# Undivided softmax probabilities, and their reciprocal sums sent through memory into the gate

## The chip, the cores and the metric

The kernel runs on one core of one Trainium2 chip. The metric is device time in microseconds, from the launch to the end of the program on the core; lower is better. The engines are TensorE (PE, with its weight loads shown as PEld), VectorE (DVE), ScalarE (ACT), GpSimd (POOL) and SyncE (SP), which here issues every DMA of the steady stage. Each engine works through its own list of instructions in order and waits on semaphores for the others.

## The reference

One encoder layer over 4096 tokens of width 1024. What matters here is the attention half: 32 blocks of 128 queries, 8 query heads that share 2 key heads, and a window of three key blocks.

```python
h = rmsnorm(x, pre_norm_g)
q, k, v, g_a, u_p, g_p = split(h @ w_in)
s = q k^T * scale + bias            # a 128-query block against 3 key blocks of 128
m = max(max(s), sink)
p = exp(s - m)
p = p / (sum(p) + exp(sink - m))    # the softmax with a sink
a = (p @ v) * silu(g_a)             # the gate
mixed = concat(a, pool(u_p) * silu(g_p)) @ w_out
out = x + rmsnorm(mixed, post_norm_g)
```

The division by the sum may stand before p @ v (on the probabilities) or after it (on the gate, since both multiply the same row). The change moves it from the one place to the other.

## The kernel before

The program has two stages. The first, to about 490 us, prepares weights, the pooling half and the gate `ga` = silu(g_a), which it writes to memory (`ga_scr`). The second, the attention stage, walks the 32 blocks from the last to the first, two blocks (a unit `u` of 256 tokens) at a time. Its middle part is a loop of 13 units, with blocks 27 to 2; blocks 31 to 28 and 1 to 0 have orders written out by hand.

Every float32 operand of TensorE is carried as two float16 numbers, a high part (a rounded copy, written by ACT) and a low part (the rest, written by DVE or POOL), and a product is three matmuls: high by high, high by low, low by high.

A block `b` has two passes, `half` 0 and 1, of four heads each. In a pass:

- `scores`: PE writes the logits of four heads into PSUM (`s`);
- `logits` (four, DVE): adds the bias and finds the row's maximum, into `p`. With the first, POOL copies the sink into one column of `p` (the sink copy, L1330);
- `exps` (four, ACT): exponentials in place, with their sums `den`;
- `denominators` (DVE): two tiny operations make `rd` = 2^14 / sum;
- `probs` (four, ACT, one head each): the high part of p * rd into `pn`; `rests` (four, DVE): the low part;
- `turn` (SP): one transposing DMA of `pn` into `pt`, which PE needs for `values` (p @ v).

`values` leaves its result in two PSUM tiles (`o`, and `p` in a bank of the general pool). `copy_o` (ACT) and `gate` (DVE, two operations, of which the second multiplies by the gate `gb`, which `load_ga` has fetched) make the attention output `at`. `sums`, `high` and `low` then form operands for seven `product`s per unit, named "11", "22", "12", "s1" to "s4", which PE multiplies with `w_out`; they accumulate in the same general PSUM banks (acc0, acc1, acc2) that `proj_k`, `proj_v` and `proj_q` use. `add`, `gain` (mostly POOL), `square` (ACT), `mean` (a tiny DVE operation and a power on POOL, `rs`), `residual` (DVE) and `store` finish a unit. `load_x` fetches 1 MB of operands for the unit after next.

What stands in which order on an engine is set by due times: each step is entered into a plan with a time, the plan is sorted by it, and each engine's list follows that order. The loop orders PE's work so: `scores(b,0)`, product "s4", `proj_k`, `proj_v`, `values(b+1)`, `scores(b,1)`, products "22", "11", "s2", "12" for an odd block; `scores(b,0)`, two projections of q, `values(b+1)`, `scores(b,1)`, two projections of q, products "s3", "s1" for an even one. `softmax(b, half, t)` enters a pass's steps:

```python
due(t + 4.5 + 0.6 * i, probs, b, half, i)
due(t + 5.1 + 0.62 * i, rests, b, half, i)
...
due(t + 7.8, turn, b, half)
```

In the even block `load_x` is due 2.1 after the second pair of q projections, which was just ahead of that pass's `turn`. The product "22" of the next odd block needs the low part `y22`, which POOL makes late in the even block's last passes, behind a `gain` and the power `rs`.

Of the kernel before, what the change touches and what calls it, by code (L numbers as in the profile page):

```python
# [8 lines left out]
F32 = mybir.dt.float32  # L9
# [125 lines left out]
def hybrid_layer(ctx: ExitStack, tc, io, out):  # L135
# [46 lines left out]
    ga_scr = dram.tile([NB, P, 4, P], F32, name="ga_scr")  # L182
    wb_scr = dram.tile([6, P, 2, D], F16, name="wb_scr")
# [1095 lines left out]
    pt, p_t, nm_t, den_t, rd_t, pn_t = {}, {}, {}, {}, {}, {}  # L1279

# [40 lines left out]
    def logits(b, half, i):  # L1321
# [20 lines left out]
    def exps(b, half, i):  # L1342
# [6 lines left out]
            scale=-1.0, accum_out=den_t[b, half][:, hh : hh + 1],  # L1349
        )  # L1350

    def denominators(b, half):
        den = den_t.pop((b, half))
        nc.vector.tensor_scalar(
            out=den, in0=den, scalar1=1.0 / P_SCALE, scalar2=None, op0=ALU.mult
        )
        nc.vector.reciprocal(rd_t[b, half], den)
# [5 lines left out]
    def probs(b, half, i):  # L1363
        nk = len(keys(b)) * P
        if i == 0:
# [3 lines left out]
        nc.scalar.activation(  # L1369
            prob_view(b, half)[:, 0, i], p_t[b, half][:, i, :nk], AF.Copy,  # L1370
            scale=rd_t[b, half][:, i : i + 1],
        )

    def rests(b, half, i):
        nk = len(keys(b)) * P
        pn4 = prob_view(b, half)
        nc.vector.scalar_tensor_tensor(  # L1377
            out=pn4[:, 1, i], in0=p_t[b, half][:, i, :nk], scalar=rd_t[b, half][:, i : i + 1],
            in1=pn4[:, 0, i], op0=ALU.mult, op1=ALU.subtract,
# [372 lines left out]

    now = [0.0]
# [439 lines left out]
```

## Time and profile before

| | |
|---|---|
| median of 3 runs | 1162.19 us (1161.15 to 1162.24) |
| the profiled execution | 1162.76 us, of which the span of its instructions is 1161.0 us |
| PE busy | 1146.3 us, 99% of the span |
| PEld busy | 873.5 us, 75% |
| DVE busy | 947.8 us, 82% |
| ACT busy | 717.7 us, 62% |
| POOL busy | 313.7 us, 27% |
| DMA, all queues | 228.36 MB, 197 GB/s on the mean |

The busy share of an engine is the share of the span in which it had an instruction in flight; matmuls overlap, so a PE that is busy 99% of the time is one that hardly ever stood still, and no more. In the timeline rows below, the columns are start (us), length (us), engine, line, operation, what it writes <- what it reads, shape and count; a bracket tells how long the engine stood idle before and for whom. `SPq` rows are DMA issues: their length is the time SP spent on the issue, not the transfer.

### The profile page before, as it was taken

How to read it: one execution, taken by the hardware profiler on the slowest of the kernel's cores; microseconds unless marked ns; L12 is line 12 of the kernel's file. 1: busy time of each engine (PE TensorE's matmuls, PEld its weight loads, DVE VectorE, ACT ScalarE, POOL GpSimd, SP SyncE). 2: the span in 40 equal slices, each digit the busy share in tenths (PEclk: the TensorE clock that was granted, in tenths of full speed). 3: DMA queues.
4: the chain of work that ended last, by engine and by line, in shares of the span. 5: the costliest groups of instructions: out<-in, count | busy, mean ns of one | idle time of the engine just before them, and what ended most of it. 6: DMA issues, size and time to landing. Idle time of an engine off the chain costs nothing. (4 is left out here: it accounts for less than half of the span.)

```text
span 1161.0 us, 32325 instructions
## 1 busy us (share of the span) xinstructions
PE 1146.3 (99%) x13420; PEld 873.5 (75%) x13420; DVE 947.8 (82%) x1875; ACT 717.7 (62%) x1485; POOL 313.7 (27%) x310
## 2 busy tenths in 40 slices
PE   8999999999999999999999999999999999999997
PEld 7998888888888888886667676576666767667653
DVE  6889988988799974568878888878887888887886
ACT  6876556536654542257676776676667677667772
POOL 0001120211111010201524433532533443353231
PEclk8999999999999999999999999999999999999999
DMA  9645575867667664299975886788777688777885
GB/s 344 217 128 180 174 259 183 285 229 238 227 190 225 206 179 134 76 289 242 250 185 144 197 211 143 200 202 177 177 196 184 148 198 215 140 196 165 178 216 143
DMA packets 301683, 228.36 MB, mean 197 GB/s; under 512 B 219568, under 2 KB 259504, under 8 KB 296928
## 3 DMA queue, kind: packets, MB, share of 16 engines
q1 hardware_dynamic: 301536, 226.30, 72.5%
q8 instruction: 105, 1.72, 0.6%
q14 instruction: 42, 0.34, 0.1%
HBM read 114.68 MB, written 60.34 MB: 151 GB/s over the span
## 5 line engine op out<-in xcount | busy, mean ns | idle before, releaser
L689 PEld LDWEIGHTS <-wq 128*128 128x128 f16 x4104 | 401.6, 98 | 50.4 <-DVE wq L310 2.6
L689 PE MATMUL y<-xt,wq 128*128 128x256 f16 x1512 | 203.3, 273 | 0.1
L1347 ACT ACTIVATE p<-p,nm 128x385 f32<-128x385 f32 (+1 forms) x256 | 152.9, 599 | 36.5 <-POOL p L1330 20.3
L1273 PE MATMUL aq<-xb,xb 128*128 128x256 f16 x1024 | 173.4, 273 | 0.2 <-DVE mo L1715 0.2
L1273 PEld LDWEIGHTS <-xb 128*128 128x128 f16 x1536 | 150.1, 98 | 26.4 <-issue 8.0
L1676 PE MATMUL ms<-wo,ys 128*128 128x512 f16 x720 | 163.7, 379 | 0.0
L1377 DVE SCALAR_TENSOR_TENSOR pn<-p,rd,pn 128x384 f16<-128x384 f32 (+1 forms) x256 | 157.6, 667 | 5.9 <-ACT pn L1369 5.9
L1336 DVE CUSTOM_DVE_ANT_0 p<-s,nt,nsink 128x384 f32<-128x384 f32 (+1 forms) x256 | 156.0, 666 | 2.0 <-PE s L1313 2.0
L1273 PE MATMUL aq<-xb,xt 128*128 128x256 f16 x512 | 139.6, 273 | 0.4 <-issue 0.4
L1369 ACT ACTIVATE pn<-p,rd 128x384 f16<-128x384 f32 (+1 forms) x256 | 134.8, 596 | 4.4 <-issue 1.1
L307 POOL TENSOR_TENSOR yt<-yt,sg 128x512 f32<-128x512 f32 (+2 forms) x32 | 51.0, 1594 | 301.6 <-DVE yt L310 214.8
L1676 PEld LDWEIGHTS <-ys 128*128 128x128 f16 x720 | 68.1, 98 | 83.9 <-POOL ys L1582 4.8
L1676 PE MATMUL m<-wo,y 128*128 128x512 f16 x540 | 121.8, 379 | 0.0
L1676 PEld LDWEIGHTS <-y 128*128 128x128 f16 x540 | 51.4, 98 | 63.5 <-ACT at L1543 2.9
L1273 PE MATMUL kv<-xb,xb 128*128 128x256 f16 x512 | 86.7, 273 | 0.0
L1710 POOL TENSOR_TENSOR mo<-mo,gpost 128x512 f32<-128x512 f32 x39 | 63.7, 1634 | 84.4 <-ACT jkb L1699 83.2
L1273 PEld LDWEIGHTS <-xt 128*128 128x128 f16 x768 | 75.1, 98 | 10.6 <-issue 0.8
L689 PE MATMUL plain<-xb,wq 128*128 128x256 f16 x576 | 68.0, 276 | 2.1 <-DVE wq L310 2.0
L1273 PE MATMUL kv<-xb,xt 128*128 128x256 f16 x256 | 69.8, 273 | 0.0
L689 PE MATMUL v<-xt,wq 128*128 128x256 f16 x504 | 68.6, 273 | 0.1
L689 PE MATMUL v<-xb,wq 128*128 128x256 f16 x504 | 68.6, 273 | 0.0
L689 PE MATMUL y<-xb,wq 128*128 128x256 f16 x504 | 68.6, 273 | 0.0
(221 smaller groups left out, 1854.3 us busy)
## 6 DMA issues: line engine op xcount, KB each, us to landing
nt<-in_xT SPq DMA_DIRECT2D x28, 512.0 KB
x_scr<-xb SPq DMA_DIRECT2D x14, 1024.0 KB
xb<-x_scr SPq DMA_DIRECT2D x14, 1024.0 KB
xr<-in_x SPq DMA_DIRECT2D x28, 512.0 KB
out<-xr SPq DMA_DIRECT2D x28, 512.0 KB
xn<-in_x SPq DMA_DIRECT2D x27, 512.0 KB
ga_scr<-cc SPq DMA_DIRECT2D x64, 128.0 KB
raw<-in_w_out SPq DMA_DIRECT2D x16, 512.0 KB
```

The costliest lines, as they stand in the source:

```text
L307: eng.tensor_tensor(out=out, in0=in0, in1=in1, op=op)
L689: nc.tensor.matmul(b[:, s], wq[:, slot[q, op], wv, s, k, :], x[:, xv, k, :], start=(first and k + s + wv + xv == 0), stop=(last and k == H ...
L1273: nc.tensor.matmul(acc, w[:, j, k, :], x[:, kh, v, kt, :], start=(n == 0), stop=(n == 3 * KT - 1),)
L1336: nc.vector.tensor_tensor_reduce(out=p_t[b, half][:, hh, :nk], in0=s_t[jj][:, gg, :nk], in1=bias[:, h, lo : lo + nk], scale=negc[:, h : h ...
L1347: nc.scalar.activation(p[:, hh, : nk + 1], p[:, hh, : nk + 1], AF.Exp, bias=nm_t[b, half][:, hh : hh + 1], scale=-1.0, accum_out=den_t[b, ...
L1369: nc.scalar.activation(prob_view(b, half)[:, 0, i], p_t[b, half][:, i, :nk], AF.Copy, scale=rd_t[b, half][:, i : i + 1],)
L1377: nc.vector.scalar_tensor_tensor(out=pn4[:, 1, i], in0=p_t[b, half][:, i, :nk], scalar=rd_t[b, half][:, i : i + 1], in1=pn4[:, 0, i], op0= ...
L1676: nc.tensor.matmul(z_t[u, tag], y[:, k, yi, :], wo[o][:, wi, k, :], start=(n == 0 and acc is None), stop=(n == 3 * HK - 1), skip_group_che ...
L1710: eng.tensor_tensor(out=mo, in0=mo, in1=gpost[:, cs], op=ALU.mult)
```

## The change

- `probs` and `rests` no longer divide: they scale the exponentials by the constant 2^14. Since no per-head scalar is left, one operation takes two heads (768 columns where there were 384), so a pass has two of each instead of four.
- The sums of both passes of a block go into one tile `den` of 8 columns. Once a block, after its second pass, DVE takes one reciprocal and transposes it in 32 x 32 pieces (`rec`); SP writes it to memory with four small DMAs (`keep_rows`, 8 partitions by 128 bytes each) and reads it back with two (`load_rows`, each a row of 2 KB repeated over 64 partitions) into `rdb`, a spare part of the tile XB0; POOL multiplies the gate `gb` by it (`divide`, 128 x 512 float32). `gate` then reads a gate that is already divided.
- The due times of `probs`, `rests` and `turn` are earlier, by 0.4, 0.1 and 0.9 us in the plan; `load_rows` is due at t + 8.0 and `divide` at t + 15.0.

```diff
+    rec = [pb1.tile([P, 32], F32, name=f"rec{i}") for i in range(2)]
+    rdb = XB0[:, 6 * D :].bitcast(F32).rearrange("p (i h q) -> p i h q", i=2, h=4)
...
-    def denominators(b, half):
-        den = den_t.pop((b, half))
-        nc.vector.tensor_scalar(
-            out=den, in0=den, scalar1=1.0 / P_SCALE, scalar2=None, op0=ALU.mult
-        )
-        nc.vector.reciprocal(rd_t[b, half], den)
+    def denominators(b):
+        nc.vector.reciprocal(rec[0][:, :NH], den_t.pop(b))
+        nc.vector.transpose(out=rec[1], in_=rec[0])
+
+    def keep_rows(b):
+        for i in range(4):
+            nc.sync.dma_start(
+                rd_scr[b, :, 32 * i : 32 * i + 32], rec[1][32 * i : 32 * i + NH, :]
+            )
+
+    def load_rows(b):
+        for g in range(2):
+            rows = rd_scr[b, 4 * g : 4 * g + 4, :].rearrange("(o h) q -> o h q", o=1)
+            nc.sync.dma_start(
+                rdb[64 * g : 64 * g + 64, b % 2], rows.to_broadcast([64, 4, P])
+            )
+
+    def divide(b):
+        ga = ga_t[b]
+        nc.gpsimd.tensor_tensor(out=ga, in0=ga, in1=rdb[:, b % 2], op=ALU.mult)
...
-        nc.scalar.activation(
-            prob_view(b, half)[:, 0, i], p_t[b, half][:, i, :nk], AF.Copy,
-            scale=rd_t[b, half][:, i : i + 1],
-        )
+        hs = slice(2 * i, 2 * i + 2)
+        nc.scalar.mul(prob_view(b, half)[:, 0, hs], p_t[b, half][:, hs, :nk], P_SCALE)
...
-            out=pn4[:, 1, i], in0=p_t[b, half][:, i, :nk], scalar=rd_t[b, half][:, i : i + 1],
-            in1=pn4[:, 0, i], op0=ALU.mult, op1=ALU.subtract,
+            out=pn4[:, 1, hs], in0=p_t[b, half][:, hs, :nk], scalar=P_SCALE,
+            in1=pn4[:, 0, hs], op0=ALU.mult, op1=ALU.subtract,
...
-            due(t + 4.5 + 0.6 * i, probs, b, half, i)
-            due(t + 5.1 + 0.62 * i, rests, b, half, i)
-        due(t + 4.3, denominators, b, half)
-        due(t + 7.8, turn, b, half)
+        for i in range(2):
+            due(t + 4.1 + 0.75 * i, probs, b, half, i)
+            due(t + 5.0 + 0.95 * i, rests, b, half, i)
+        if half:
+            due(t + 4.3, denominators, b)
+            due(t + 4.9, keep_rows, b)
+            due(t + 8.0, load_rows, b)
+            due(t + 15.0, divide, b)
+        due(t + 6.9, turn, b, half)
```

The hand-written orders at both ends get the same steps, with `load_rows` due at the later of 0.1 after `turn` and 2.5 after `denominators`, and `divide` 2.5 after that.

Three places show what the change does to the order. The first is SP's list in the second pass of an even block (here block 20 of unit 10), from the `turn` of its first pass (`pt20_0`) to the `turn` of the next block (`pt19_0`); `xr` are the residual's inputs, `gb20` the gate, `xb1<-x_scr` is `load_x`. Before:

```order
L1386 DMA_TRANSPOSE pt20_0_10490<-pn20_0_10355 128x24x128
L1723 DMA xr22_10492<-in_x 128x1024
L1723 DMA xr23_10494<-in_x 128x1024
L1460 DMA gb20_10554<-ga_scr_97 128x512
L1259 DMA xb1_68<-x_scr_95 128x4096
L1386 DMA_TRANSPOSE pt20_1_10593<-pn20_1_10568 128x24x128
L1743 DMA out_0<-xr22_10492 128x1024
L1386 DMA_TRANSPOSE pt19_0_10767<-pn19_0_10723 128x24x128
```

And the same place of SP's list after the change:

```order
L1403 DMA_TRANSPOSE pt20_0_10369<-pn20_0_10287 128x24x128
L1745 DMA xr22_10423<-in_x 128x1024
L1745 DMA xr23_10425<-in_x 128x1024
L1482 DMA gb20_10483<-ga_scr_97 128x512
L1362 DMA rd_scr_98<-rec1_6088 8x32 x4
L1403 DMA_TRANSPOSE pt20_1_10521<-pn20_1_10492 128x24x128
L1260 DMA xb1_68<-x_scr_95 128x4096
L1369 DMA xb0_66<-rd_scr_98 64x512 x2
L1765 DMA out_0<-xr22_10423 128x1024
L1403 DMA_TRANSPOSE pt19_0_10687<-pn19_0_10652 128x24x128
```

The four small writes come in ahead of the `turn`; `load_x`, which stood ahead of it, now stands behind it, and the two `load_rows` stand behind `load_x`.

The second place is POOL's list from the sink copy of block 19's first pass to the low part `y12` (unit 11 is being finished, unit 10 prepared). Before:

```order
L1330 COPY p19_0_10677<-nsink_87 128x4
L1710 TENSOR_TENSOR mo11_1_10179<-mo11_1_10179,gpost_6084 128x512
L1733 TENSOR_TENSOR rs11_1_10715<-ms11_1_10713,mhalf_72 128x1
L1710 TENSOR_TENSOR mo11_0_10178<-mo11_0_10178,gpost_6084 128x512
L1733 TENSOR_TENSOR rs11_0_10759<-ms11_0_10757,mhalf_72 128x1
L1582 TENSOR_TENSOR y22_10_10762<-yf0_10_10224,y22_10_10762 128x4x128
L1582 TENSOR_TENSOR y12_10_10764<-yf1_10_10343,y12_10_10764 128x4x128
```

POOL's list at the same place after the change (`gb20<-gb20,xb0` is the `divide` of block 20; `xb0` holds `rdb`):

```order
L1333 COPY p19_0_10607<-nsink_87 128x4
L1732 TENSOR_TENSOR mo11_1_10116<-mo11_1_10116,gpost_6085 128x512
L1755 TENSOR_TENSOR rs11_1_10645<-ms11_1_10643,mhalf_72 128x1
L1375 TENSOR_TENSOR gb20_10483<-gb20_10483,xb0_66 128x512
L1732 TENSOR_TENSOR mo11_0_10115<-mo11_0_10115,gpost_6085 128x512
L1755 TENSOR_TENSOR rs11_0_10685<-ms11_0_10683,mhalf_72 128x1
L1604 TENSOR_TENSOR y22_10_10689<-yf0_10_10161,y22_10_10689 128x4x128
L1604 TENSOR_TENSOR y12_10_10691<-yf1_10_10279,y12_10_10691 128x4x128
```

The `divide`, which waits for the two `load_rows`, has come in ahead of a `gain`, a power and the low parts `y22` and `y12`.

The third place is ACT's list in both passes of block 20, from the exponentials of the first to the `probs` of the second. Before:

```order
L1347 ACTIVATE p20_0_10338,den20_0_10336<-p20_0_10338,nm20_0_10335 128x385 x4
L1262 ACTIVATE q9_0_10352<-aq9_0_10285 128x512
L1369 ACTIVATE pn20_0_10355<-p20_0_10338,rd20_0_10337 128x384 x4
L1543 ACTIVATE at21_10438<-o21_10360,gaf_78 128x512
L1578 CAST y11_10_10496<-at21_10438 128x4x128
L1347 ACTIVATE p20_1_10550,den20_1_10548<-p20_1_10550,nm20_1_10547 128x385 x4
L1262 ACTIVATE q9_1_10565<-aq9_1_10498 128x512
L1369 ACTIVATE pn20_1_10568<-p20_1_10550,rd20_1_10549 128x384 x4
```

ACT's list there after the change:

```order
L1350 ACTIVATE p20_0_10274,den20_10273<-p20_0_10274,nm20_0_10272 128x385 x4
L1388 ACTIVATE pn20_0_10287<-p20_0_10274 128x768
L1263 ACTIVATE q9_0_10289<-aq9_0_10222 128x512
L1388 ACTIVATE pn20_0_10287<-p20_0_10274 128x768
L1565 ACTIVATE at21_10371<-o21_10295,gaf_78 128x512
L1600 CAST y11_10_10427<-at21_10371 128x4x128
L1350 ACTIVATE p20_1_10479,den20_10273<-p20_1_10479,nm20_1_10478 128x385 x4
L1388 ACTIVATE pn20_1_10492<-p20_1_10479 128x768
L1263 ACTIVATE q9_1_10496<-aq9_1_10429 128x512
L1388 ACTIVATE pn20_1_10492<-p20_1_10479 128x768
```

The first `probs` of each pass has gone ahead of `keep_q`'s high part (`q9<-aq9`, which reads the PSUM bank of a q projection); before, that stood ahead of all four.

More of the change, by code (lines that the diff above doesn't have):

```diff
@@ L182, in hybrid_layer @@
     ga_scr = dram.tile([NB, P, 4, P], F32, name="ga_scr")
+    rd_scr = dram.tile([NB, NH, P], F32, name="rd_scr")
     wb_scr = dram.tile([6, P, 2, D], F16, name="wb_scr")
@@ L1326, in logits @@
             nm_t[b, half] = pb.tile([P, 4], F32, name=f"nm{b}_{half}", tag="nm")
-            den_t[b, half] = pb.tile([P, 4], F32, name=f"den{b}_{half}", tag="den")
-            rd_t[b, half] = pb.tile([P, 4], F32, name=f"rd{b}_{half}", tag="rd")
+            if half == 0:
+                den_t[b] = pb.tile([P, NH], F32, name=f"den{b}", tag="den")
             p = p_t[b, half] = pb.tile([P, 4, 3 * P + 1], F32, name=f"p{b}_{half}", tag="p")
@@ L1348, in exps @@
             p[:, hh, : nk + 1], p[:, hh, : nk + 1], AF.Exp, bias=nm_t[b, half][:, hh : hh + 1],
-            scale=-1.0, accum_out=den_t[b, half][:, hh : hh + 1],
-        )
-    def denominators(b, half):
-        den = den_t.pop((b, half))
-        nc.vector.tensor_scalar(
-            out=den, in0=den, scalar1=1.0 / P_SCALE, scalar2=None, op0=ALU.mult
-        )
-        nc.vector.reciprocal(rd_t[b, half], den)
+            scale=-1.0,
+            accum_out=den_t[b][:, 4 * gg + 2 * half + jj : 4 * gg + 2 * half + jj + 1],
+        )
+    def denominators(b):
[15 more added lines that the diff above has]
+        nc.gpsimd.tensor_tensor(out=ga, in0=ga, in1=rdb[:, b % 2], op=ALU.mult)
     def prob_view(b, half):
@@ L1376, in rests @@
         pn4 = prob_view(b, half)
+        hs = slice(2 * i, 2 * i + 2)
         nc.vector.scalar_tensor_tensor(
-            out=pn4[:, 1, i], in0=p_t[b, half][:, i, :nk], scalar=rd_t[b, half][:, i : i + 1],
-            in1=pn4[:, 0, i], op0=ALU.mult, op1=ALU.subtract,
+            out=pn4[:, 1, hs], in0=p_t[b, half][:, hs, :nk], scalar=P_SCALE,
+            in1=pn4[:, 0, hs], op0=ALU.mult, op1=ALU.subtract,
         )
@@ L1751, in load_gain @@
         )
+    due(-1.0, nc.vector.memset, rec[0], 0.0)
     now = [0.0]
@@ L1849, in soft @@
             at_(te + 0.65 * i, exps, b, half, i)
-            at_(tp + 0.55 * i, probs, b, half, i)
-            at_(tr + 0.62 * i, rests, b, half, i)
-        at_(td, denominators, b, half)
+        for i in range(2):
+            at_(tp + 0.8 * i, probs, b, half, i)
+            at_(tr + 0.95 * i, rests, b, half, i)
+        if half:
+            at_(td, denominators, b)
+            at_(td + 0.4, keep_rows, b)
+            at_(max(tt + 0.1, td + 2.5), load_rows, b)
+            at_(max(tt + 2.6, td + 5.0), divide, b)
         at_(tt, turn, b, half)
```

## The prediction

> **What bounds the kernel now.** I read the page's busy line first, then the list of PE's waits, then the timeline of one unit of the loop (blocks 21 and 20, about 699.9 to 741.3 us), since all 13 units look alike.
>
> ```profile
> span 1161.0 us, 32325 instructions
> PE 1146.3 (99%) x13420; PEld 873.5 (75%) x13420; DVE 947.8 (82%) x1875; ACT 717.7 (62%) x1485; POOL 313.7 (27%) x310
> ...
> PE o L1483 <- DMA pt<-pn: 1.5, 2, 0.8
> PE z L1648 <- DVE xb L1715: 0.6, 1, 0.6
> PE aq L1273 <- issue: 0.4, 1, 0.4
> PE aq L1273 <- DVE mo L1715: 0.2, 1, 0.2
> PE o L1513 <- DMA pt<-pn: 0.2, 1, 0.2
> ```
>
> The waits are in total us, times, longest. The attention stage has 1.5 + 0.6 + 0.4 + 0.2 + 0.2 = 2.9 us of them in 670 us. So PE sets the time, and the change alters no matmul. What it saves on ACT and DVE can be worth at most those 2.9 us; what it costs is whatever makes PE wait. The question is therefore how much slack each product has that depends on a step that moves.
>
> ```profile
> 699.94 5.35 PE L1676 MATMUL m<-wo,y 128*128 128x512 f16 x24
> ...
> 724.58 5.34 PE L1676 MATMUL ms<-wo,ys 128*128 128x512 f16 x24
> 729.85 0.93 PE L1313 MATMUL s<-k_all,q 64*32 64x288 f16 x48
> 730.71 2.76 PE L1676 MATMUL ms<-wo,ys 128*128 128x512 f16 x12
> ...
> 741.27 4.06 PE L1676 MATMUL m<-wo,y 128*128 128x512 f16 x18
> ```
>
> A unit runs from 699.94 to 741.27, 41.3 us. The products "s3" and "s1" start at 724.58 (12 matmuls each, so "s1" at 724.58 + 2.63 = 727.21), "s4" at 730.71, and "22" of the next unit at 741.27.
>
> **The change part by part.** *Wider operations* (columns: busy us, mean ns of one, idle before).
>
> ```profile
> L1369 ACT ACTIVATE pn<-p,rd 128x384 f16<-128x384 f32 x240 | 128.0, 603 | 3.1 <-issue 1.1 <-ACT p L1347 1.0 <-ACT k_all L1262 0.2
> L1369 ACT ACTIVATE pn<-p,rd 128x256 f16<-128x256 f32 x16 | 6.8, 497 | 1.3 <-DVE rd L1357 0.8 <-ACT jkb L1699 0.4
> L1377 DVE SCALAR_TENSOR_TENSOR pn<-p,rd,pn 128x384 f16<-128x384 f32 x240 | 150.3, 677 | 4.0 <-ACT pn L1369 4.0
> L1377 DVE SCALAR_TENSOR_TENSOR pn<-p,rd,pn 128x256 f16<-128x256 f32 x16 | 7.3, 511 | 1.9 <-ACT pn L1369 1.9
> L1357 DVE RECIPROCAL rd<-den 128x4 f32<-128x4 f32 x64 | 11.4, 178 | 2.2
> L1354 DVE TENSOR_SCALAR den<-den 128x4 f32<-128x4 f32 x64 | 10.7, 168 | 65.2 <-ACT p L1347 65.2
> L455 DVE STREAM_TRANSPOSE turned<-turned x5: 211/211/213, 143.4 to 340.4; 128x32 f32<-128x32 f32 x5
> ```
>
> On ACT the step from 256 to 384 columns costs (603 - 497) / 128 = 0.83 ns a column, so 768 columns take 603 + 318 = 921 ns: 285 ns saved for each of 120 pairs, and as much for 8 shorter ones, 36 us. On DVE 1.30 ns a column gives 1175 ns, 179 ns saved a pair, 23 us with the short ones; the 64 scalings go (10.7 us), 32 of 64 reciprocals go (5.7), 32 transposes come (6.8). ACT falls to about 682 us, DVE to about 915. PE waits for neither, so I count 0; if a pass did become late, this is what would make it earlier, by 0.3 to 0.6 us.
>
> *The order on ACT: first `probs` ahead of `keep_q`.*
>
> ```profile
> 718.12 2.21 DVE L1377 SCALAR_TENSOR_TENSOR pn<-p,rd,pn 128x384 f16<-128x384 f32 x4
> 720.27 0.75 DVE L1551 SCALAR_TENSOR_TENSOR at<-p,gaf,at 128x512 f32<-128x512 f32 x1
> ...
> 724.85 0.57 ACT L1262 ACTIVATE q<-aq 128x512 f16<-128x512 f32 x1
> ...
> 725.46 0.69 DVE L1263 SCALAR_TENSOR_TENSOR q<-aq,q 128x512 f16<-128x512 f32 x1
> 729.96 0.69 DVE L1715 TENSOR_TENSOR mo<-ms,mo 128x512 f32<-128x512 f32 x1
> ```
>
> In block 20's first pass the low part of q and hence the two `rests` start about 0.85 us later (921 ns less an overlap of some 0.09); four `rests` took 2.2 us, 0.55 each where the mean row says 0.677; in the same proportion two long ones take 1.9, so the `gate` at 720.27 comes about 0.5 us late. DVE then starts the second pass's logits 0.5 late, ACT its exponentials, and again one `probs` stands ahead of `keep_q`: its low part, at 725.46 before, starts at 725.46 + 0.5 + 0.85 = 726.8 and ends at 727.45. "s1" writes the PSUM bank that this operation reads, and is due at 727.21: PE waits 0.3. The following `rests` and `add`s are shifted likewise; the `add` of 729.96 ended at 730.65, just before "s4" (730.71), which accumulates into the bank that it reads: there is no slack, and I take 0.3 more. Bounds: 0, if the shorter work wins the delay back, and 0.85 + 0.5 less the 1.0 us of slack before "s1", plus the same for "s4", 1.0. I take 0.6 a unit, for 12 units with both steps: 7 us.
>
> *SP: `keep_rows` and `load_rows`.* The nearest row to a small write is the one of stage one that has the same shape of job:
>
> ```profile
> L459 SPq DMA_DIRECT2D rs_scr<-turned x20: 483/485/602, 143.6 to 342.3; - x20
> 724.08 1.06 SPq L1723 DMA_DIRECT2D xr<-in_x  x2
> 725.67 0.43 SPq L1259 DMA_DIRECT2D xb<-x_scr  x1
> 729.87 4.54 SPq L1386 DMA_TRANSPOSE pt<-pn  x1
> ```
>
> Four issues of 0.49 us are 2 us of SP per block, between the transpose (about 725.9) and the `turn`, which cannot start before the last `rests`, near 730: hidden. The writes themselves lie behind `xr` in the queue, but have 4 us. The `turn` stays where it was (729.95 against 729.87: `rests` end no earlier, being later by the order and shorter by their width). `load_x`, at 725.67 before, now waits behind it: at 729.95 + 4.2 = 734.15, and the two `load_rows` are issued from 734.6 to 735.5. `load_x` itself is needed only a unit later, so its delay costs nothing. But the rows queue behind its 1 MB. What the queue does is seen in windows of 1 us (the last two columns are the share of the DMA engines and GB/s):
>
> ```profile
> 727.00:728.00 1.00, 1.00 (x6) 0.44 (x5) 0.87 (x2) 0.57 (x2) 0.00 (x0) 1.00 1.01 397
> 730.00:731.00 1.00, 1.00 (x50) 0.62 (x35) 1.00 (x2) 0.26 (x1) 1.00 (x2) 1.00 1.00 385
> 735.00:736.00 1.00, 1.00 (x11) 0.90 (x10) 0.97 (x1) 1.00 (x4) 0.91 (x1) 1.00 1.18 269
> 736.00:737.00 1.00, 1.00 (x11) 0.90 (x10) 1.00 (x2) 1.00 (x4) 1.00 (x1) 1.00 0.00 0
> ```
>
> While `xr`, `gb` and `load_x` drain back to back the rate is 0.39 MB per us with all engines busy; the `turn` issued until 734.41 has moved its last byte by 736.0, 1.6 us later. So after the change: `turn` through at 735.8, `load_x` (1.05 MB, 2.7 us) at 738.5, the rows (0.26 MB, 0.7 us) at 739.2, and with 0.4 for the completion POOL can go at about 739.6. Bounds: 738.6 (issue 3.6 us instead of 4.2 and no completion time) and 740.8 (half the rate for the rows and the `turn`'s 4.54).
>
> *POOL: `divide` in a queue that PE waits for.*
>
> ```profile
> 734.46 0.54 POOL L1733 TENSOR_TENSOR rs<-ms,mhalf 128x1 f32<-128x1 f32 x1 [1.65 <-DVE den L1354]
> 735.10 2.36 POOL L1710 TENSOR_TENSOR mo<-mo,gpost 128x512 f32<-128x512 f32 x1
> 739.19 0.85 POOL L1733 TENSOR_TENSOR rs<-ms,mhalf 128x1 f32<-128x1 f32 x1 [1.74 <-DVE ms L1728]
> 740.01 2.27 POOL L1582 TENSOR_TENSOR y<-yf,y 128x512 f16<-128x512 f32 x2
> ...
> 742.02 0.81 DVE L1555 TENSOR_TENSOR at<-at,gb 128x512 f32<-128x512 f32 x1
> 731.54 1.27 POOL L1710 TENSOR_TENSOR mo<-mo,gpost 128x512 f32<-128x512 f32 x1 [0.43 <-ACT jkb L1699]
> ```
>
> Before, the `gain` of 735.10 ran early, and `y22` (the first of the two at 740.01) ended at 741.15, right before its product at 741.27. Now `divide` stands ahead of that `gain`, and POOL can start nothing until 739.6. Then, one behind the other: `divide` 1.3 (the multiplication of the same size at 731.54), `gain` 1.4, power 0.7, `y22` 1.15: 744.15. PE is due at 741.27 + 0.6 = 741.9 and needs the low part with its third matmul, 0.44 later, at 742.3. With 0.15 for the semaphore PE waits 2.0 us. The gate itself (742.02) gets its factor at 740.9, in time. In the odd block no `load_x` stands between, so the rows land some 3 us earlier relative to POOL's idle stretch and nothing waits. `load_x` is issued in 11 units (it has nothing left to fetch in the last two of the loop): 11 x 2.0 = 22 us. Bounds: 0.6 (rows at 738.6 and quiet POOL operations) and 4.2 (rows at 740.8 and one of the two multiplications at 2.36), so 7 to 46 us.
>
> The 2.36 against 1.27 of the same multiplication is a matter of company: at 735.10 DVE ran `residual` and `rests`, with two SBUF inputs each, at 731.54 the logits, with one input in PSUM. [...]
>
> *The end.* The last `divide` stands in POOL's list ahead of the powers for unit 1, on which a `residual` waits on DVE, and behind that the last `gate`. No row prices it; between 0 and a `divide` with its wait, 4 us; I take 2, nearer to one `divide` of 1.3.
>
> Sum: 0 + 7 + 22 + 2 = 31 us on the profiled execution's 1162.76 us, that is 1193.8; the median of the runs lies 0.57 lower, so 1193.
>
> **Rivals.**
>
> *Half rate for the rows.* Each `load_rows` reaches 64 of the 128 partitions. If such a transfer runs on half of the queue's paths, the two take 2 x 0.131 / 0.195 = 1.34 us instead of 0.7, POOL starts 0.65 later, and 11 units lose 7 us more: 1200. The trace has no load of 64 partitions, so nothing in it speaks for or against. [...]
>
> *Everything heavier.* If the rows come past 741, the gate waits too, and with it the sums, `s2` and the logits behind them; 4.2 us a unit is 46 + 7 + 2, 1217.
>
> *`divide` is hidden.* If POOL can go by 737.6, the chain ends at 737.6 + 4.55 = 742.15 and PE does not wait for it; the order on ACT and the end remain: 1162 + 7 + 2, 1171.
>
> *No change.* As before, and the earlier `rests` win back the 0.6: 1162.
>
> *Faster.* If nothing waits and the passes are earlier by 0.5 us, PE's two waits for `pt` at the start of the stage (1.5 us) and the one of 0.6 at the end go: 1160. It needs POOL to go by 737.0 (the product is then due at 741.27 again), 2.6 us sooner than I have it, in every unit, and the 0.6 of ACT's order won back; the 1 MB ahead of them speaks against it.
>
> **How the numbers follow.** Chances: my forecast 0.47, half rate 0.22, heavier 0.11, `divide` hidden 0.11, no change 0.05, faster 0.04. 0.2% (2.3 us) is about what a measurement can tell here. Slower holds the first four, 0.91; same 0.05; faster 0.04. The range reaches from just above `divide` hidden, 1172, to between half rate and heavier, 1211; about a fifth is left outside.
>
> **What would show it.** In the trace after: a wait of PE's weight loads for POOL's `y` of about 2 us, eleven times, at the start of "22"; POOL idle before the `divide`, ended by the DMA of the rows, some 4 us long in every even block and hardly in the odd ones; ACT near 682 us, DVE near 915; PE busy as before but a share of 96%; small waits of "s1" and "s4". I am wrong if POOL's idle before `divide` is ended early enough (no PE wait for `y`), or if PE waits for `gate` or `pt` instead.

## The result: 5.5% slower, twice the loss that was predicted

After the change the median of 4 runs is 1226.63 us (1223.42 to 1229.83), beside 1162.22 us for the kernel before on the same chip: a ratio of 1.0554, 95% interval 1.0519 to 1.0589, or +64.4 us. Predicted were +31 us and a range from 1172 to 1211. The profiled execution is the one of 1223.42 us; the four runs differ with the mean granted clock, which is 0.986 at 1223.42 and 1224.46 us, 0.981 at 1228.81 and 0.979 at 1229.83.

From the page after, and then from its list of PE's waits (total us, times, longest):

```profile
span 1221.6 us, 32332 instructions
PE 1158.2 (95%) x13420; PEld 875.1 (72%) x13420; DVE 925.1 (76%) x1684; ACT 679.6 (56%) x1357; POOL 355.2 (29%) x342
```

```profile
PE m L1698 <- POOL y L1604: 39.0, 13, 4.7
PE kv L1274 <- DVE q L1264: 2.5, 1, 2.5
```

ACT and DVE became lighter nearly as forecast (682 and 915 us were forecast, 679.6 and 925.1 measured), and PE now waits 39.0 us for the low part of y, where the list of before had no such row. One unit from the timeline after, blocks 21 and 20 again; first SP (the `turn`, `load_x`, the two `load_rows`), then POOL, DVE and PE:

```profile
713.88 3.65 SPq L1403 DMA_TRANSPOSE pt<-pn  x1
717.63 0.53 SPq L1260 DMA_DIRECT2D xb<-x_scr  x1
718.35 1.90 SPq L1369 DMA_DIRECT2D xb<-rd_scr  x2
...
719.24 0.54 POOL L1755 TENSOR_TENSOR rs<-ms,mhalf 128x1 f32<-128x1 f32 x1 [1.36 <-DVE ms L1750]
725.04 1.27 POOL L1375 TENSOR_TENSOR gb<-gb,xb 128x512 f32<-128x512 f32 x1 [5.26 <-DMA xb<-rd_scr]
726.27 1.27 POOL L1732 TENSOR_TENSOR mo<-mo,gpost 128x512 f32<-128x512 f32 x1
727.49 1.00 POOL L1755 TENSOR_TENSOR rs<-ms,mhalf 128x1 f32<-128x1 f32 x1
728.46 2.92 POOL L1604 TENSOR_TENSOR y<-yf,y 128x512 f16<-128x512 f32 x2
...
726.88 1.21 DVE L1577 TENSOR_TENSOR at<-at,gb 128x512 f32<-128x512 f32 x1
...
726.05 0.60 PE L1698 MATMUL m<-wo,y 128*128 128x512 f16 x2
729.88 6.61 PE L1698 MATMUL m<-wo,y 128*128 128x512 f16 x22 [3.22 <-POOL y L1604]
```

The rows (what `load_rows` fetches) stand behind `load_x`. POOL, idle since 719.78, gets them at 725.04, and `divide`, `gain`, `rs` and `y22` follow one behind the other; PE does two matmuls of "22" and stands 3.22 us. So far this is the prediction's picture. But the 22 matmuls that follow take 6.61 us, where 24 took 5.35 before. Here are windows of one length of this unit and of the one two later (columns: stretch, length, then busy us of PE, PEld, DVE, ACT and POOL with their instructions, granted clock, DMA share, GB/s):

```profile
727.80:731.20 3.40, 1.32 (x7) 0.62 (x8) 3.30 (x4) 0.00 (x0) 3.40 (x3) 1.00 0.79 162
731.20:734.60 3.40, 3.40 (x10) 1.20 (x9) 3.13 (x9) 2.60 (x8) 2.72 (x4) 0.50 0.00 0
...
820.00:823.40 3.40, 1.71 (x8) 0.80 (x9) 3.33 (x3) 0.00 (x0) 3.40 (x4) 1.00 0.67 137
823.40:826.80 3.40, 3.40 (x17) 1.57 (x16) 2.73 (x9) 2.99 (x9) 2.72 (x3) 1.00 0.00 0
```

At half the granted clock 10 matmuls fall into 3.4 us instead of 17. In this execution it happens behind the first 5 waits of the loop (6.8 us long behind the first of them) and behind none of the later ones; the windows before and after 800 us differ accordingly:

```profile
500.00:800.00 300.00, 274.85 (x3697) 184.14 (x3696) 206.64 (x425) 166.58 (x401) 110.63 (x113) 0.96 0.80 191
800.00:1160.00 360.00, 339.46 (x4598) 225.38 (x4597) 271.14 (x532) 213.25 (x506) 159.81 (x154) 1.00 0.76 183
```

A mean of 0.96 over 300 us is 24 us at half clock, up to 12 us lost. Of these, 3.4 us at half clock lie ahead of the loop, at 529.8, behind a wait of 2.5 us for q; 20.5 us lie in the loop, so up to 10.2 us are lost there.

Where the time went is seen by the starts of "22". The first "22" of the loop starts at 575.7 us in the trace before and at 584.0 after; twelve units on, the thirteenth starts at 1072.2 and at 1128.5. Of the 60.7 us between the two profiled executions, 8.3 are lost ahead of the loop, 48.0 in these twelve units and 4.3 behind them. The 48.0 are 37.0 of waits for y and about 10 of half clock, and less than 1 us of anything else.

### The profile page after: what moved, and what is told of

The parts are those of the page before. It is cut to its first block, busy times and chain, and to the rows that moved or that the text cites. A ratio compares the mean times of both kernels' runs of the same rounds, so it can differ in the third digit from the quotient of the medians.

```text
span 1221.6 us, 32332 instructions
## 1 busy us (share of the span) xinstructions
PE 1158.2 (95%) x13420; PEld 875.1 (72%) x13420; DVE 925.1 (76%) x1684; ACT 679.6 (56%) x1357; POOL 355.2 (29%) x342
## 3 DMA queue, kind: packets, MB, share of 16 engines
q8 instruction: 105, 1.72, 0.6%
## 5 line engine op out<-in xcount | busy, mean ns | idle before, releaser
L1698 PE MATMUL m<-wo,y 128*128 128x512 f16 x540 | 133.4, 400 | 40.1 <-POOL y L1604 39.0
L1394 DVE SCALAR_TENSOR_TENSOR pn<-p,pn 128x768 f16<-128x768 f32 (+1 forms) x128 | 121.7, 980 | 10.7 <-ACT pn L1388 10.6
L1388 ACT ACTIVATE pn<-p 128x768 f16<-128x768 f32 (+1 forms) x128 | 102.5, 819 | 0.0
L1375 POOL TENSOR_TENSOR gb<-gb,xb 128x512 f32<-128x512 f32 x32 | 41.4, 1294 | 148.9 <-DMA xb<-rd_scr 145.1
L1732 POOL TENSOR_TENSOR mo<-mo,gpost 128x512 f32<-128x512 f32 x39 | 50.4, 1292 | 90.3 <-ACT jkb L1721 90.3
L1264 DVE SCALAR_TENSOR_TENSOR q<-aq,q 128x512 f16<-128x512 f32 x31 | 21.4, 692 | 66.5 <-ACT q L1263 66.4
```

What stands on the lines that cost most here:

```text
L1264: nc.vector.scalar_tensor_tensor(out=dst_l, in0=acc, scalar=QKV_EVAC, in1=dst_h, op0=ALU.mult, op1=ALU.subtract)
L1375: nc.gpsimd.tensor_tensor(out=ga, in0=ga, in1=rdb[:, b % 2], op=ALU.mult)
L1388: nc.scalar.mul(prob_view(b, half)[:, 0, hs], p_t[b, half][:, hs, :nk], P_SCALE)
L1394: nc.vector.scalar_tensor_tensor(out=pn4[:, 1, hs], in0=p_t[b, half][:, hs, :nk], scalar=P_SCALE, in1=pn4[:, 0, hs], op0=ALU.mult, op1=ALU ...
L1698: nc.tensor.matmul(z_t[u, tag], y[:, k, yi, :], wo[o][:, wi, k, :], start=(n == 0 and acc is None), stop=(n == 3 * HK - 1), skip_group_che ...
L1732: eng.tensor_tensor(out=mo, in0=mo, in1=gpost[:, cs], op=ALU.mult)
```

## The experiments

Times are medians of 4 to 10 runs; the kernel before, run beside them, stayed between 1162.0 and 1163.1 us. The theory to start with: the rows come late by their place in SP's list, POOL's list hands this on to y, and the clock adds to each wait. "The trip" stands below for `keep_rows`, `load_rows` and `divide` together.

**Which part costs what: leaving out.** e12 leaves out `divide`, e6 also `keep_rows` and `load_rows`; e7 is e6 with the first `probs` behind `keep_q`. The same lines go from the hand-written orders. The gate is not divided in these three.

```diff
-            due(t + 4.1 + 0.75 * i, probs, b, half, i)      # e7 only
+            due(t + 4.35 + 0.75 * i, probs, b, half, i)
-            due(t + 4.9, keep_rows, b)                       # e6, e7
-            due(t + 8.0, load_rows, b)                       # e6, e7
-            due(t + 15.0, divide, b)                         # e12, e6, e7
```

> The changed kernel without divide: the sums still go to memory and the rows come back, behind the turn and load_x as in the change, but nothing reads them (the gate is not divided). Theory (in the loop only POOL's wait passes the lateness on; SP's part costs at the ends alone, where load_rows holds the turn): 1162 + 8 = 1170, between 1163 and 1177, no half clock in the loop. Rival (SP's standing and the traffic cost PE directly, through late turns): above 1185.

> The changed kernel without the way through memory: keep_rows, load_rows and divide are left out (so the gate is not divided); the operations over two heads, their order, the shared reciprocal and load_x's place stay. Theory (rows and divide cause the waits for y and ys, the half clock, and most of what start and end lose; the ACT order the rest, 0.9 x 12 = 11): 1162.2 + 11 + 2 = 1175, between 1168 and 1184. Rival (the wide operations themselves make DVE and ACT late at the wrong places, and the 38 us that e1 left are theirs): 1190 to 1203.

> As e6, and with the first probs behind keep_q on ACT as in e5: what the wide operations bring or cost alone. Theory (nothing: ACT and DVE have time, PE has 3 us of waits to give at most): 1163, between 1160 and 1168. Rival (an operation over two heads holds DVE or ACT too long somewhere in the loop, for over 0.5 us a unit): above 1169.

Measured: e12 1170.80 us (ratio 1.0071, 1.0056 to 1.0086), e6 1162.20 (0.9998, 0.9989 to 1.0008), e7 1158.05 (0.9970, 0.9957 to 0.9982). So the 64 us are 55.8 for `divide` on POOL, 8.6 for the rows' way through SP, and 0 for the rest, in which the wide operations gain about 4 and the order on ACT gives them back. e12 is as expected. e6 and e7 came out below their ranges: alone, the order costs 4 us, not 11, and the wide operations gain where nothing was expected. In the loop a unit of e6 takes 41.55 us where e7 has 41.25; the 0.3 are lost in "s2". Of the 7.7 us between the profiled executions of e12 and e6, 6.8 lie ahead of the loop's first "22". PE's longest wait in e12, then SP's rows of e12 there (transposes, L1362 `keep_rows`, L1369 `load_rows`), and both of e6:

```profile
PE o L1504 <- DMA pt<-pn: 6.9, 2, 4.7
```

```profile
511.30 1.30 SPq L1362 DMA_DIRECT2D rd_scr<-rec  x4
513.05 3.73 SPq L1403 DMA_TRANSPOSE pt<-pn  x1
518.26 1.15 SPq L1369 DMA_DIRECT2D xb<-rd_scr  x2
...
521.37 8.04 SPq L1403 DMA_TRANSPOSE pt<-pn  x1
532.11 4.97 SPq L1403 DMA_TRANSPOSE pt<-pn  x1
```

```profile
PE o L1502 <- DMA pt<-pn: 1.6, 1, 1.6
```

```profile
520.44 5.30 SPq L1403 DMA_TRANSPOSE pt<-pn  x1
527.67 6.36 SPq L1403 DMA_TRANSPOSE pt<-pn  x1
```

In e12 SP stands from 516.78 to 518.26 at `load_rows`, until `keep_rows`, issued behind a 1 MB load of `wo`, has landed; the third `turn` begins 0.9 us later than in e6 and holds SP for 8.04 us instead of 5.30, and the fourth goes out at 532.11 instead of 527.67. `values` waits 4.7 us for it, and the clock is at half behind that wait, which counts in the 8.6:

```profile
537.40:544.20 6.80, 4.17 (x53) 2.60 (x53) 2.08 (x7) 2.67 (x6) 0.00 (x0) 0.50 1.13 288
```

Why the third `turn` took 8.04 us was not tried apart.

**The rows' place and `divide`'s place: e1, e4.** e1 moves `load_x` behind `load_rows`, e4 moves `divide` of the even blocks behind y12.

```diff
-            due(now[0] + 2.1, load_x, u - 3)                 # e1
+            due(now[0] + 3.4, load_x, u - 3)
-            due(t + 15.0, divide, b)                         # e4
+            due(t + (15.0 if b % 2 or b == 2 else 20.5), divide, b)
```

> The changed kernel with one row of SP's list moved: in the loop load_x is issued behind the two load_rows instead of ahead of them. Theory (POOL's divide waits for rows that queue behind 1 MB): the rows land 4 to 4.5 us earlier, y22 is ready at least 1 us before PE needs it, and the 11 waits of the loop for y (about 35 of 39.0 us) go, and with them the stretches at half clock behind them (some 24 us at half clock, 12 us lost): 1226.6 - 35 - 12 = 1180, between 1172 and 1188, granted clock back to the 0.99 of the kernel before. [...] Rival (half rate of rows to 64 partitions): rows land, but 0.7 us later than by the theory; no more than 8 us above it.

> The changed kernel with divide moved on POOL, in the even blocks, from ahead of gain, rs, y22 and y12 to behind them; SP's order stays, the rows come as late as before. Theory (it is divide's place in POOL's queue that hands the rows' lateness to y22): no wait of PE for y in the loop, no half clock, -47 us; the gate now waits for divide (rows 1.5 us after y12, divide 1.3), some 1.5 us late on DVE, and what it costs PE is open between 0 and 1.6 us x 12: 1180 to 1199, I take 1185. Rival (the gate's lateness is passed on in full to s2 and the logits, with their own half clock): above 1200.

Measured: e1 1200.88 us (1.0328, 1.0311 to 1.0345), e4 1202.58 (1.0346, 1.0330 to 1.0361). Both take the large waits away, and neither reaches its expectation. PE's wait for y in e1, and a `divide` of an even block in its timeline:

```profile
PE m L1698 <- POOL y L1604: 9.0, 10, 4.2
```

```profile
931.14 1.83 POOL L1375 TENSOR_TENSOR gb<-gb,xb 128x512 f32<-128x512 f32 x1 [2.35 <-DMA xb<-rd_scr]
```

POOL's idle time ahead of `divide` fell from 5.26 to 2.35 us and PE's waits for y from 39.0 to 9.0. What stayed was small and everywhere: by the starts of successive matmuls in one unit of e1, 0.4 us lost in "22", 0.9 in "s2", up to 0.7 in "s3" and "s1", 0.2 behind them; in e4, 0.6 and 1.1 in the first two. In the changed kernel itself "s2" and the products behind it lose nearly nothing: these losses were hidden behind the wait for y. So the place of the rows is shown, but it is 26 us of the 56, not 47.

**Order on ACT: e5** (e1 with the first `probs` as in e7).

> The kernel of e1 (load_x behind load_rows) with the first probs of a pass due 0.25 later, so that on ACT it stands behind keep_q as before the change; nothing else moves. In e1 PE's record shows in each unit 0.7 us lost in s3 and s1 and 0.2 in the scores behind them, waits for DVE's low part of q. Theory (the prediction's term for the order on ACT, 0.6 us a unit; 0.9 by e1): these go in 12 units, 1200.9 - 11 = 1190, between 1187 and 1194. Rival (they come from divide's lateness, as the rest does): no change, 1199 to 1203.

Measured: 1191.65 us (1.0254, 1.0239 to 1.0269), 9.2 less than e1; the losses in "s3" and "s1" are gone from its matmul starts. As expected.

**Only a wait, or more than one: e2.** "11" and "22" change places on PE.

> The changed kernel with two products swapped on PE: 11 before 22, so that 22 needs its y 2.6 us later; the other engines keep their order. Theory (one wait of PE for y22 per unit, 3.0 us on the mean, and the clock behind it): the wait shrinks to 0.4 us a unit on the mean, 12 units x 2.6 = 31 us less, no half clock, 12 us less: about 1183, between 1175 and 1192. Rival (y22 is only the first of several things that the rows make late, the gate and the products behind it too): PE waits as long a little later, and the time stays above 1205.

Measured: 1213.38 us (1.0439, 1.0423 to 1.0455). It is a miss, and the theory of one single wait fell here, as the rival had it. The wait for y fell to 5.2 us, but others took its place:

```profile
PE m L1698 <- DVE at L1573: 8.2, 12, 0.7
PE ms L1698 <- POOL ys L1604: 7.0, 11, 0.6
```

The late POOL work makes the gate and "s2" late too, hidden before behind the wait for y.

**The clock: e3, e16.** e3 fills PE's wait in the changed kernel, e16 makes a wait in the kernel before.

```diff
+        due(now[0], fill, u, 10)                             # e3, ahead of each "22"; in fill, 10 times:
+            nc.tensor.matmul(
+                z_t[u, 2], wo[OT4][:, 0, 0, :P], wo[OT4][:, 0, 1, :], start=True, stop=True,
+                skip_group_check=True,
+            )
...
+            for _ in range(4):                               # e16, ahead of y22's low part
+                due(t0 + 8.7, more)       # gpsimd multiplication of a spare 128 x 512 tile
```

> The changed kernel with ten more matmuls (on weights that are always there, 2.2 us) on PE right ahead of each 22 of the loop, into the bank that 22 then overwrites. They take up waiting time, so PE has work but the end of the wait stays where POOL sets it. Theory (behind the longer waits the clock is granted at half for 3.4 us, which costs 1.7 us each time): no stretch at half clock in the loop, waits for y of 0.8 us instead of 3.0, time 1226.6 - 12 = 1214, between 1210 and 1219. Rival (the half clock in the records costs nothing, or comes from something else): the time stays at 1225 to 1229, or the half-clock stretches remain.

> The kernel before, and nothing of the change: in the loop four more multiplications of 128 x 512 float32 on POOL (1.27 us each, on a spare tile) right ahead of y22. PE's slack there is 0.5 us, so it waits 4 x 1.27 - 0.5 = 4.6 us for y in each of 13 units, 60 us. Theory (a wait of that length leaves most of a window of 3.4 us idle, so a stretch at half clock of at least 3.4 us follows each, 1.7 us lost): 1162 + 60 + 22 = 1244, granted clock near 0.97. Rival (the clock falls for another reason in the changed kernel, and a wait costs its length): 1222.

Measured: e3 1218.69 us (1.0486, 1.0471 to 1.0502), e16 1246.85 (1.0722, 1.0706 to 1.0738). In e3 waits of 12.7 and 13 x 2.16 us of filling replace the 39.0 of waits, the mean clock from 500 to 800 us is 0.99 where it was 0.96, and the time falls by 7.9, into the expected range. Behind the loop's waits for y no stretch at half clock is left; one stays at 584.9, behind a wait of 2.35 us for `pt` just ahead of the first "22". In e16, which came as its theory had it, all 13 waits are alike; their sum, and windows of one unit (the wait, the first 3.4 us behind it, the rest):

```profile
PE m L1677 <- POOL y L1583: 62.3, 13, 4.8
```

```profile
768.00:773.00 5.00, 0.21 (x2) 0.01 (x1) 4.86 (x5) 0.00 (x0) 4.84 (x5) 1.00 0.97 203
773.10:776.50 3.40, 3.40 (x9) 1.18 (x9) 2.78 (x9) 2.45 (x8) 3.40 (x4) 0.50 0.02 5
776.60:815.80 39.20, 39.20 (x556) 26.77 (x554) 28.83 (x65) 26.05 (x63) 13.23 (x15) 1.00 0.68 169
```

The 83.8 us over the kernel before (1163.10 beside it) are 62.3 of waiting and 21.5 more, on the mean 1.65 for each of 13 stretches at half clock (eleven of 3.4 us, two of 6.8). So a wait costs its length and, if a stretch follows, some 1.7 us beside. Where a stretch begins is seen in the trace after: its six drops between 500 and 1200 us (529.85, 587.87, 635.66, 683.45, 731.23 and 775.61) lie whole multiples of 3.413 us apart, and each stretch is one or two such steps long. Of the steps at full clock, the one ahead of each drop has PE busy for 0.00 to 1.35 us, every other one for 1.65 us or more. So a step need not be idle: PE was busy in 1.32 of 3.40 us in the window ahead of the drop at 731.2, while no drop followed at 823.4 on a window with 1.71. Waits of about 3 us, shorter than a step, cost more than their length where a drop follows, by e3 7.9 us in all.

**What stays when the rows are early: e8, e10, e11, e13.** e8 is e5 with `load_rows` ahead of the even block's `turn`; e10 does so in both blocks and sends the loads of `xr` ahead of the first pass's `turn`; e11 is the changed kernel, with `load_x` in its old place, the first `probs` behind `keep_q`, `xr` as in e10 and `load_rows` issued from ACT; e13 is e5 with y22 and y12 ahead of `gain`.

```diff
-            due(t + 8.0, load_rows, b)
+            due(t + (8.0 if b % 2 else 6.85), load_rows, b)  # e8; e10: 6.85 for both
-            due(t0 + 9.0, load_xr, u + 1, 1)                 # e10, e11, both loads
+            due(t0 + 2.1, load_xr, u + 1, 1)
+            nc.scalar.dma_start(rdb[...], rows)              # e11, due t + 10.2 (odd), 7.5 (even)
-            pair(t0 + 8.1, u + 1, "22", a22)                 # e13, and "12" from 8.7 to 4.3
+            pair(t0 + 4.2, u + 1, "22", a22)
```

> As e5, and in the even blocks load_rows stands ahead of the turn on SP, so that the rows queue behind neither load_x nor the turn. Theory (every late row of e1 comes from SP's queue; what divide then costs POOL fits into its idle time): POOL starts divide some 3 us earlier than in e1, the 0.4 for y and 0.9 for ys go in 12 units, 1190 - 16 = 1174, between 1169 and 1181; what stays over 1162 is start and end. Rival (SP stands still until keep_rows has landed, so the turn comes 1 to 3 us later and values waits for pt instead): above 1188.

> As e5, and in the loop the two loads of xr (1 MB) go ahead of the first pass's turn instead of ahead of keep_rows, and load_rows goes ahead of the second pass's turn in both blocks. Theory (in e8 keep_rows landed 4.5 us after its issue because it queued behind xr, and SP stood until then; with xr away the writes land 1 us after issue and the rows 4 to 5 us earlier than in e8): no wait of PE for y, ys or pt in the loop beyond 0.2 us a unit, what stays is start and end: 1191.7 - 13 = 1178, between 1173 and 1183. Rival (divide on POOL costs by its presence, since it and DVE's two-input operations hold each other up): s2 stays 0.5 us late in every unit, 1184 to 1190.

> The changed kernel with load_rows issued by ACT, on a DMA queue of its own, after the second pass's probs, with the first probs behind keep_q and xr early as in e10; load_x stays ahead of the turn's rows on SP. Theory (what makes the rows late is their place in SP's list and queue, behind the turn and load_x; on a queue of their own they land some 3 us after issue whatever SP does, and SP never stands for keep_rows, at the ends neither): 1162 + 8 = 1170, between 1162 and 1179. Rival (the DMA engines are shared, so the rows are as late as before beside load_x, or ACT stands for keep_rows and the exponentials with it): above 1185.

> As e5, and the operands y22 and y12 are made earlier: on POOL straight behind divide, ahead of gain and rs; their high parts on ACT ahead of the first pass's probs. Theory (in e5 each unit loses 0.4 in 22 because y ends a chain divide, gain, rs, y, and 0.5 in s2 because that y then runs beside DVE's gate, which takes 1.07 us instead of 0.75 on the mean): both go in 12 units, 1191.7 - 11 = 1181, between 1178 and 1185. Rival (rs and the residual behind it become late instead, or DVE is late for another reason): 1188 to 1195.

Measured: e8 1190.19 us (1.0244, 1.0227 to 1.0261), e10 1197.28 (1.0296, 1.0276 to 1.0316), e11 1208.00 (1.0389, 1.0352 to 1.0426), e13 1191.08 (1.0246, 1.0219 to 1.0273): four misses. e8 shows SP standing, as its rival had it (the `keep_rows` of one even block, and the `load_rows` that waits for it):

```profile
738.25 1.06 SPq L1745 DMA_DIRECT2D xr<-in_x  x2
739.36 0.43 SPq L1482 DMA_DIRECT2D gb<-ga_scr  x1
739.89 1.31 SPq L1362 DMA_DIRECT2D rd_scr<-rec  x4
745.72 1.10 SPq L1369 DMA_DIRECT2D xb<-rd_scr  x2
```

In e10 and e11 the waits for y are gone from the list, but PE waits for `pt`, 14.1 and 18.9 us in all, of which 6.6 and 6.9 lie in the hand-written ends. `xr` now follows the odd block's `turn`; whether that makes the waits, and whether they are the whole of the loss, was not tried apart. In all four "s2" is still 0.5 to 0.8 us late in most units. The reason is in DVE's rows. Two units of e13: in each, the gate's second operation (L1577), the sum that reads it (L1633) and POOL's `gain` (L1732), in order of time; and then the same gate operation in e7, where POOL is done with y in time:

```profile
713.37 0.72 DVE L1577 TENSOR_TENSOR at<-at,gb 128x512 f32<-128x512 f32 x1
713.50 1.72 POOL L1732 TENSOR_TENSOR mo<-mo,gpost 128x512 f32<-128x512 f32 x1
714.13 1.64 DVE L1633 TENSOR_TENSOR s<-at,yf 128x512 f32<-128x512 f32 x1
...
755.72 1.26 POOL L1732 TENSOR_TENSOR mo<-mo,gpost 128x512 f32<-128x512 f32 x1
756.02 1.50 DVE L1577 TENSOR_TENSOR at<-at,gb 128x512 f32<-128x512 f32 x1
757.56 0.69 DVE L1633 TENSOR_TENSOR s<-at,yf 128x512 f32<-128x512 f32 x1
```

```profile
745.03 0.70 DVE L1574 TENSOR_TENSOR at<-at,gb 128x512 f32<-128x512 f32 x1
```

In these rows the operation that starts second is the slow one: `gain` takes 1.72 us behind the gate at 713.37 and then slows the sum, and where `gain` starts first, at 755.72, the gate takes 1.50. Either way DVE's chain to "s2" is 0.8 to 1.0 us longer in the unit.

**Ends as before, POOL quiet at the gate: e9, e14, e15, e17, e18.** e9 is e5 without the trip in blocks 31 to 28, 1 and 0, whose gates then stay undivided; in e14 these blocks divide their probabilities as before the change, so that all is divided; e15 is e14 with e13; e17 is e14 with blocks 3 and 2 as before too, and `gain` and `rs` behind ys2's low part; e18 is e17 with e13.

```diff
+    def old(b):                                              # e14, e15, (b < 4: e17, e18)
+        return b < 2 or b >= NB - 4
-        due(t + 1.4, gain, u, 0, HI)                         # e17, e18
-        due(t + 4.0, mean, u, 0)
+        due(t + 9.8, gain, u, 0, HI)
+        due(t + 10.4, mean, u, 0)
```

> As e5 (load_x behind load_rows, first probs behind keep_q), but keep_rows, load_rows and divide are left out for the six blocks of the hand-written orders at both ends and for block 28 (their gates are not divided); the loop keeps them. Theory (by PE's record of e5, the first 22 of the loop starts 10 us later than in the kernel before, and the last two units take 4 us longer; both come from the trip at the ends, where load_rows holds SP and the turn behind it): 1191.7 - 10 - 4 = 1178, between 1173 and 1183. Rival (the start's loss is only slack that the loop takes back): above 1186.

> As e5, but the blocks of the hand-written orders and block 28 divide their probabilities as before the change, one head per operation, with no trip; the loop's 26 blocks keep the change. All is divided. Theory (the trip at the ends costs 17 us, by e9 against e5; dividing there as before costs some 3 us of what e7 gained): 1177, between 1173 and 1181. Rival (the changeover between the two ways makes a pass late): above 1183.

> e13 and e14 together, a complete kernel: rows ahead of load_x, probs behind keep_q, y early, old ends. If both theories hold: 1191.7 - 11 - 15 = 1166, between 1161 and 1172; it beats the kernel before only if the loop also keeps the 0.1 us a unit of e7. Rival (e13 does nothing): 1177.

> As e14 (rows ahead of load_x, probs behind keep_q, ends divided as before, now blocks 3 and 2 too), and the gain and rs that stood between divide and y22 on POOL go behind ys2's low part, so that POOL has no multiplication left that can run beside the gate. Theory (DVE's gate takes 0.75 us again once POOL is quiet beside it, and y is early): the 0.9 us a unit go in 12 units, 1176 - 11 - 2 = 1163, between 1160 and 1168. Rival (y still ends beside the gate, or rs makes the residual late on DVE instead): 1172 to 1180.

> e17, and y22 and y12 with their high parts earlier on ACT as in e13, so that y is surely done before the gate. Theory: as e17, 1163, or up to 2 us less where y still met the gate there. Rival (the high parts ahead of probs make the first pass's turn late on SP): 2 to 6 us more than e17.

Measured: e9 1174.23 us (1.0102, 1.0086 to 1.0119), e14 1176.33 (1.0117, 1.0102 to 1.0132), e15 1179.23 (1.0142, 1.0125 to 1.0159), e17 1189.32 (1.0241, 1.0223 to 1.0260), e18 1194.18 (1.0279, 1.0253 to 1.0305). e9 and e14 hold: the trip in these blocks costs 15 to 17 us. Most of that is at the start: in the profiled executions of e5 and e14 the loop's first "22" starts at 585.3 and 575.0. e15 and e18 are misses, both where their rivals had them (e13's change does nothing; 2 to 6 us more than e17, 4.9 measured). e17's time is a miss beyond its rival too, but its trace answers the question; the groups of e17 (mean ns), then the same of e7, then PE's waits in e17 and one `residual` of e17 (L1792) with POOL's row beside it:

```profile
L1610 DVE TENSOR_TENSOR at<-at,gb 128x512 f32<-128x512 f32 x25 | 17.3, 692 | 4.4 <-POOL gb L1389 1.8 <-DVE at L1606 0.5
L1792 DVE SCALAR_TENSOR_TENSOR xr<-mo,rs,xr 128x1024 f32<-128x1024 f32 x28 | 48.2, 1722 | 7.9 <-POOL rs L1788 7.8
```

```profile
L1574 DVE TENSOR_TENSOR at<-at,gb 128x512 f32<-128x512 f32 x25 | 17.5, 701 | 0.9
L1756 DVE SCALAR_TENSOR_TENSOR xr<-mo,rs,xr 128x1024 f32<-128x1024 f32 x28 | 35.6, 1273 | 8.5 <-POOL rs L1752 8.5
```

```profile
PE aq L1274 <- DVE mo L1770: 19.7, 12, 2.8
```

```profile
710.67 1.28 POOL L1675 TENSOR_TENSOR yf<-yf,at 128x512 f32<-128x512 f32 x1
710.80 2.22 DVE L1792 SCALAR_TENSOR_TENSOR xr<-mo,rs,xr 128x1024 f32<-128x1024 f32 x1
```

With POOL quiet beside it the gate takes 692 ns in the loop, and no wait for y is left; "s2" takes 2.62 us from its first matmul to that of "12", where e14 has 3.14 in most units and e7 2.59. So POOL's company was the cause of the lateness of "s2". But `residual` now waits for the later `gain` and `rs`, and one of POOL's `sums` starts just ahead of it: once a unit it takes 2.22 us (1722 ns on the mean of all, 1273 in e7), the `rests` behind it are late, and PE waits 19.7 us for an `add`. The slow operation is again the one that started second. No complete version beat the kernel before; the nearest is e14, 13.2 us above the kernel before beside it.

## Why the prediction was wrong

The direction and the place were right: ACT and DVE gave PE little, `divide` stands in a queue that PE waits for, y22 is late and the gate is hardly waited for (1.1 us in all). The step that failed is the size of `divide`'s term: the prediction put the wait at 2.0 us in 11 units, 22 us, and gave the clock behind the waits no term. Measured are 39.0 us of waits and about 10 us of half clock in the loop; leaving out `divide` alone gives back 55.8 us (e12). Step by step:

- *Wider operations, 0.* e7 measures -4.0 beside its kernel before (interval -2.1 to -5.0), so the bound of 2.9 us is not excluded. Its one profiled execution is the slowest of ten, 1163.14 us, so no trace shows where the 4 us were gained. In the profile after, 768 columns take 832 ns on ACT, where 921 were worked out, and 995 on DVE, where 1175 were.
- *Order on ACT, 7.* The changed kernel does not pay it: behind the long wait for y, PE's list has one wait of 0.5 us for the low part of q in a product. It shows when that wait is gone: 4.1 alone (e6 less e7, and there in "s2"), 9.2 beside late rows (e1 less e5, in "s1" as the sum had it, and in "s2"). The terms do not add up; that 7 lies between the two is luck.
- *SP, hidden.* Right in the loop, where e12 has no loss beyond e6. Wrong in the hand-written start, which the prediction did not look at: 8.6 us, SP standing at `load_rows`, with the clock behind it.
- *`divide` on POOL, 2.0 x 11 = 22.* The step that failed. The waits of 39.0 are 13 and not 11, since the first "22" of the loop stands behind a `load_x` of the hand-written start (4.2 us) and one more lies in the hand-written end (2.0); the 11 between have 32.8, so 3.0 each and not 2.0. In these 11 units, on the mean, `divide` gets its rows 5.0 us after SP has issued them, where the sum had 4.1, so it starts 1.2 us before "22" and not 2.3; the four operations from there to y22 take 4.8 us instead of 4.55 (`rs` 1.00 instead of 0.7). What holds the rows was not tried apart; the sum did not count the `store` of 0.5 MB that SP issues right behind them. No row shows its 0.4 us for the completion and 0.15 for the semaphore; in the unit shown PE goes on 0.06 us behind the end of y22.
- *The clock* had no term at all: 7.9 us by e3, about 10 in the loop by the trace. The profile of before shows no wait in the loop, so no row there could price it. The rival "everything heavier" (1217) came nearer in time, but not by its mechanism, a wait for the gate.
- *POOL's company.* The prediction had the row (2.36 against 1.27 us) and took the quiet price. In the changed kernel `gain` was indeed quiet (1.27 at 726.27). The cost comes on the other side, and it reaches PE only where the long wait is gone: DVE's gate, 1.50 us for 0.70 in e13, `residual` 2.22 for 1.27 in e17. Beside the gate ran POOL's `gain` (1.26 us), beside `residual` one of its `sums` (1.28 us); the rows do not show by what one holds up the other. This company is a part of the 13.2 us that e14 still has over the kernel before: on the mean 0.4 us a unit in "s2", beside 0.3 in "22", where y itself ends late behind `divide`.
- *The ends, 2.* Measured are 4.3 us behind the loop, and 8.3 ahead of it, where the sum had nothing. By e14 against e5 the trip in the hand-written blocks costs 15 us.

Undone one behind the other, the +64.4 are 25.8 for `load_x` ahead of the rows with its clock (e1), 9.2 for the order on ACT (e5), 15.3 for the ends (e14), and about 14 that stay with `divide` on POOL in the loop. Another order of undoing gives other shares, as the 4.1 for the order on ACT show. The rival of half rate for 64 partitions was not singled out by any run. e11's `load_rows` on a queue of their own with `xr` in its old place was not tried.

## What to carry to other kernels

Where PE is busy 99%, a step added to an engine that is busy 27% still had three prices here: the waits that it hands on from its own operand (39.0 us), the clock behind long waits of PE (about 10), and, once the waits were gone, the company that it gives to the operations beside it (0.4 us a unit in "s2"). Such prices did not add up here: the long wait hid the small ones until it was removed. A DMA that reads what another has written held its issuing queue here until the first had landed (4.5 us in e8), and whatever was issued ahead of the first counted. Price the hand-written ends of a pipeline apart from its loop.

## What the runs showed of the hardware that was not expected

- The granted clock halves for 3.4 us behind some waits of about 3 us and not behind others: a window with 1.32 of 3.40 us busy was followed by half clock, one with 1.71 was not. The length of the wait alone does not decide: in the trace after, a wait of 2.74 us (775.72) was followed by half clock, one of 3.42 (1043.51) was not. Each stretch cost 1.65 us on the mean (e16). In e16, with waits of 4.8 us, it came behind every one.
- A two-input operation of DVE and a multiplication of POOL that overlap did not share the loss: the one that started second was longer, 1.72 us for 1.27 on POOL or 1.50 for 0.70 on DVE, in two units of one run (e13).
- Four writes of 1 KB held SP for 4.5 us when 1 MB of `xr` had been issued ahead of them (e8: issued by 741.20, `load_rows` at 745.72), and for 1.8 us without it (e10, its timeline of SP):

```profile
960.81 1.32 SPq L1362 DMA_DIRECT2D rd_scr<-rec  x4
963.90 1.11 SPq L1369 DMA_DIRECT2D xb<-rd_scr  x2
```
